# RMSNorm and matmul: TensorE's instructions put in a loop of sixteen tiles, pairs of tiles in three PSUM banks

## The chip, the cores and the metric

The kernel runs on one core of a Trainium2 chip. The metric is the device time of one execution in microseconds; the figure given is the median of the runs. A profile shows one execution, from its first to its last instruction. TensorE (PE) multiplies matrices and writes its results to PSUM. VectorE (DVE) and ScalarE (ACT) work on SBUF and read PSUM. GpSimd (POOL) works on SBUF. SyncE (SP) only issues transfers here. Sixteen DMA engines carry every transfer between DRAM and SBUF, and also the engines' instructions.

## The reference

```python
batch, seq, dim, out_dim = 16, 1024, 512, 768
rms = np.sqrt(np.mean(x ** 2, axis=-1, keepdims=True) + eps)
x_norm = x / rms * gamma
return np.matmul(x_norm, weight).astype(np.float32)
```

`x` is (16, 1024, 512), `weight` (512, 768), all float32. So 33.6 MB of x are read and 50.3 MB of result are written.

## The kernel before, in words

The 16384 rows are 128 tiles of 128 rows, and two tiles are a pair `j` (0 to 63). `gamma` is multiplied into the weights once, which become `w_bf` in bfloat16. The division by the root mean square is left to the end: the product of the raw x and `w_bf` is multiplied by `rstd`, one number a row.

The path of a tile:

- SP loads x in groups of 16 tiles (`load`, line 174; some groups as two transfers of 8) into one of two buffers `xt`. `load_until` is called at the top of each pair and issues a group's load when the pair is 17 or fewer pairs short of it; in SP's order it stands behind the store ahead of it.
- ACT squares and sums each tile (`square`, line 189) and takes the root for a group of pairs (`root`, line 198); DVE takes the reciprocal.
- POOL casts x to bfloat16 (`cast`, line 184, into `xb`).
- PE transposes the tile, two bfloat16 as one 32-bit word, 2 words a tile (`transpose_word`, line 225) into one of the two PSUM banks 6 and 7 (`tp`). It does so for the pair two ahead, in between the products of the present pair (`feeder`, line 324). DVE copies the result to `xT` (`evac`, line 234). The last four tiles of each group of 16 from the second on (a "quad") go another way: POOL casts them into `xq`, and DVE transposes blocks of 32 x 32 from there into `xTq` in 16 moves (`cast_quad` and `move_quad`, three moves a pair). So in six of eight pairs PE has four transposes beside its products, and in two it has none.
- PE multiplies: for each of 4 slices of the features one weight load of `xT` (`hold`, line 294) and two products against `w_bf`, 512 and 256 columns wide (`product`, line 297; `matmuls`, line 305). The result of one tile takes two PSUM banks, one of them half used. Three such accumulators (banks 0 to 5, `ops`) are used in turn, so a tile waits for the scaling of the tile three before it.
- ACT scales the even tiles and DVE the odd ones from PSUM into `ot` (`finish_tile`, line 316; `scale`, line 276). `ot` has three buffers of 8 tiles.
- SP stores 8 tiles as one transfer of 3 MB (`store`, line 287); the first and last groups are split. The scaling of a store's last tile waits for that of the tile before it, so that the store has one wait.

What sets the order: every operation is added to a list with the names of what it reads and writes (`Order.add`). `Order.emit` (line 39) goes through the list once, finds for each operation on whom it must wait, gives each engine one semaphore that counts its awaited operations and each transfer one of a few others, and issues all operations in list order. Each engine runs its own operations in that order, fully written out: TensorE's stream has all 128 tiles in it. The loop over pairs starts in line 404, and its last lines are

```python
for i, engine in ((2 * j, ACT), (2 * j + 1, DVE)):
    a = accumulator()
    matmuls(i, a, range(K), feed)
    finish_tile(i, a, engine)
```

Of the kernel before, what the change touches and what calls it, by code (L numbers as in the profile page):

```python
# [11 lines left out]
F32 = mybir.dt.float32  # L12
BF16 = mybir.dt.bfloat16
# [3 lines left out]
P = 128  # L17
# [3 lines left out]
class Order:  # L21
# [1 line left out]

    def __init__(self, tc):  # L30
        self.tc, self.ops = tc, []

    def add(self, proc, engine, issue, reads=(), writes=()):
        self.ops.append((proc, engine, issue, list(reads), list(writes)))

    def transfer(self, engine, issue, reads=(), writes=()):
# [1 line left out]

    def emit(self):
        nc = self.tc.nc  # L40
        streams = {id(e): n for n, e in enumerate((nc.tensor, nc.vector, nc.scalar, nc.gpsimd, nc.sync))}
        writer, readers = {}, {}
        known = [dict() for _ in streams]
        clocks, needs, place, slot_of, slots = [], [], [], {}, []
        count = [0] * len(streams)
        for n, (proc, engine, _, reads, writes) in enumerate(self.ops):
            at = streams[id(engine)]
            if proc is None:
                me, turn = ("transfer", n), 1
            else:  # L50
                count[at] += 1
                me, turn = at, count[at]
            written = {writer[cell] for cell in reads + writes if cell in writer}
            read = {d for cell in writes for d in readers.get(cell, ())}
            need = []
            for d in sorted(written | read, reverse=True):
                who, when = place[d]
                if who == me and (engine is nc.tensor or d not in written):
                    continue
                if known[at].get(who, 0) < when:  # L60
                    need.append(d)
                    for k, v in clocks[d].items():
                        known[at][k] = max(known[at].get(k, 0), v)
            if proc is None:
                free = [k for k, d in enumerate(slots) if known[at].get(("transfer", d), 0)]
                if free:
                    slots[free[0]] = n
                else:
                    slots.append(n)
                slot_of[n] = ("slot", slots.index(n))  # L70
            clock = dict(known[at])
            clock[me] = turn
            place.append((me, turn))
            clocks.append(clock)
            needs.append(need)
            for cell in reads:
                readers.setdefault(cell, []).append(n)
            for cell in writes:
                writer[cell], readers[cell] = n, []
        awaited = {d for need in needs for d in need}  # L80
        seen = {who for clock in known for who in clock}
        last = [n for n, (me, _) in enumerate(place) if me not in seen and not isinstance(me, int)]
        sems, marks, done = {}, {}, {}
        for n in range(len(self.ops)):
            me = slot_of.get(n, place[n][0])
            if n in slot_of or n in awaited:
                if me not in sems:
                    sems[me] = self.tc.alloc_semaphore(f"done{len(sems)}")
                done[me] = done.get(me, 0) + (16 if n in slot_of else 1)
                marks[n] = (sems[me], done[me])  # L90
        for n, (proc, engine, issue, _, _) in enumerate(self.ops[:-1]):
            for d in needs[n]:
                engine.wait_ge(*marks[d])  # L93
            ins = issue()
            if n in marks:
                ins.then_inc(marks[n][0], 16 if n in slot_of else 1)
        return [marks[n] for n in last if n < len(self.ops) - 1], self.ops[-1][2]


@with_exitstack  # L100
def kernel(
# [9 lines left out]
    PE, DVE, ACT, POOL, SP = nc.tensor, nc.vector, nc.scalar, nc.gpsimd, nc.sync  # L111
    order = Order(tc)

    def run(engine, issue, reads=(), writes=()):
        order.add(1, engine, issue, reads, writes)

    x = x.flatten_outer_dims()
    out = out.flatten_outer_dims()
# [36 lines left out]
    xb = [sb(f"xb{n}", [P, 8, D], BF16) for n in range(2)]  # L155
    jk = [sb(f"jk{n}", [P, D], BF16) for n in range(2)]
    xT = [sb(f"xT{n}", [P, 2, 2, P, 2], BF16) for n in range(4)]
    xq = [sb(f"xq{n}", [P, 4, D], BF16) for n in range(2)]
    xTq = [sb(f"xTq{n}", [P, 4, 2, P, 2], BF16) for n in range(2)]
    ot = [sb(f"ot{n}", [P, OG, O], F32) for n in range(3)]  # L160
    ssq = sb("ssq", [P, NT], F32)
    rms = sb("rms", [P, NT], F32)
    rstd = sb("rstd", [P, NT], F32)
    psum = nc.alloc_psum_tensor("ps", [P, 8 * WIDE], F32).ap()
    ops = [psum[:, 2 * WIDE * n:2 * WIDE * (n + 1)] for n in range(3)]
    tp = [psum[:, WIDE * n:WIDE * (n + 1)].rearrange("p (t h m) -> p t h m", t=2, h=2) for n in (6, 7)]

    def cells(name, slot, i, n=1):
# [65 lines left out]
    def evac(j, t=0, n=2):  # L234
        b = bank(j, t)
        src = tp[b].rearrange("p t h m -> p t (h m)").bitcast(BF16)
        dst = xT[j % 4].rearrange("p t h m c -> p t (h m c)")
        run(DVE, lambda: DVE.tensor_copy(out=dst[:, t:t + n, :], in_=src[:, t:t + n, :]),  # L238
            [("tp", b)], cells("xT", j % 4, t, n))
        for a in range(t, t + n):  # L240
            xT_of[2 * j + a] = (xT[j % 4][:, a], ("xT", j % 4, a))

    def transpose_tile(i):
        for h in range(2):
# [10 lines left out]

    def cast_quad(q):
        src, of = x_of(4 * q, 4)
        s = 4 * q // XG % 2
        run(POOL, lambda: POOL.tensor_copy(out=xq[s], in_=src), of, [("xq", s)])  # L259
        for t in range(4):  # L260
            xT_of[4 * q + t] = (xTq[s][:, t], ("xTq", s))
        words = xq[s].rearrange("p t d -> p (t d)").bitcast(F32).rearrange("p (a w) -> p a w", w=P)
        turned = xTq[s].rearrange("p t h m c -> p (t h m c)").bitcast(F32).rearrange("p (a m) -> p a m", m=P)
        for tokens in range(0, P, B):
            for features in range(0, P, B):
                quad_moves.append((turned[features:features + B, :, tokens:tokens + B],
                                   words[tokens:tokens + B, :, features:features + B], s))

    def move(dst, src, s):
        run(DVE, lambda: DVE.transpose(out=dst, in_=src), [("xq", s)], [("xTq", s)])  # L270

    def move_quad(n):
        for _ in range(min(n, len(quad_moves))):
# [5 lines left out]
        else:  # L279
            run(DVE, lambda: DVE.tensor_single_scalar(out=dst, in_=src, scalar=r, op=mybir.AluOpType.mult), reads, writes)  # L280

    turns = iter(range(NT + 1))

    def accumulator():
        return next(turns) % 3

    def store(i):
        first, n = o_first[i], o_size[i]
# [8 lines left out]
    def product(dst, lhsT, rhs, start, stop, reads, writes):  # L297

        run(PE, lambda: PE.add_instruction(mybir.InstMatmult(  # L299
            name=nc.get_next_instruction_name(), engine=mybir.EngineType.PE,  # L300
            ins=[PE.lower_ap(rhs), PE.lower_ap(lhsT)], outs=[PE.lower_ap(dst)],
            start_tensor_calc=start, stop_tensor_calc=stop, tile_size=(P, P), tile_position=(0, 0), ldweights=False)),
            reads, writes)

    def matmuls(i, a, ks, feed=None):
        block, cell = xT_of[i]
        for k in ks:
            lhsT = block[:, k // 2, :, k % 2]
            hold(lhsT, cell)
            for half, lo, hi in ((0, 0, WIDE), (1, WIDE, O)):  # L310
                product(ops[a][:, lo:hi], lhsT, w_bf[:, k, lo:hi], k == 0, k == K - 1,
                        [cell, ("w", k, half)], [("ops", a, half)])
            if feed:
                feed()

    def finish_tile(i, a, engine):
        s = i // OG % 3

        before = [("ot", s, i % OG - 1)] if i == o_first[i] + o_size[i] - 1 else []
        scale(engine, ot[s][:, i % OG, :], ops[a][:, :O], rstd[:, i:i + 1],  # L320
              [("ops", a, 0), ("ops", a, 1), ("rstd", i)] + before, [("ot", s, i % OG)])
        store(i)

    def feeder(pairs, gaps, alone=False):
# [18 lines left out]
    def load_weights(h):  # L343
# [10 lines left out]
    run(POOL, lambda: POOL.memset(ident_f, 0.0), [], ["ident"])  # L354
    run(POOL, lambda: POOL.affine_select(out=ident_f, in_=ident_f, compare_op=mybir.AluOpType.not_equal, fill=1.0, base=0,
                                         pattern=[[-1, P]], channel_multiplier=1), ["ident"], ["ident"])
    spare = accumulator()

    def warm_up(n):
        hold(warm[:, :P], "warm")  # L360
        for _ in range(n):
            product(ops[spare][:, :WIDE], warm[:, :P], warm, True, True, ["warm"], [("ops", spare, 0)])

    def weights(k, engine, lo=0, hi=O):
        halves = [half for half in range(2) if lo <= half * WIDE < hi]
# [19 lines left out]
    weights(0, DVE, 0, WIDE)  # L385
    weights(0, DVE, WIDE, O)
    weights(1, ACT)
    acc = [accumulator() for _ in range(2)]
    for i in range(2):
        matmuls(i, acc[i], [0, 1])  # L390
    weights(2, DVE)
    weights(3, ACT)
    norms(2, 2)
    cast(4, 2)
    matmuls(0, acc[0], [2, 3])
    finish_tile(0, acc[0], ACT)
    matmuls(1, acc[1], [2, 3], feeder([1], [2, 2], alone=True))
    finish_tile(1, acc[1], DVE)
    cast(6, 2)


# [2 lines left out]
    for j in range(1, NP):  # L404
# [20 lines left out]
            feed = feeder([j + 2], two)  # L425
        else:
            feed = None
        for i, engine in ((2 * j, ACT), (2 * j + 1, DVE)):
            a = accumulator()
            matmuls(i, a, range(K), feed)  # L430
            finish_tile(i, a, engine)


    with tc.tile_critical():  # L434
# [45 lines left out]
```

## Time and profile before

| what | value |
|---|---|
| median of 3 runs | 209.27 us (208.94 to 209.97) |
| profiled execution, first to last instruction | 207.5 us |
| TensorE busy, granted clock | 193.3 us (93%), 0.992 |
| DVE, ACT, POOL busy | 149.3, 144.5, 59.8 us |
| DMA, data queue's share of 16 engines | 97.3%, 85.46 MB |
| DMA, instruction queues | 7 packets and 0.11 MB; 5 packets and 0.04 MB |

The profiled execution's own time outside the profile is not given; its span is 1.77 us under the median of the runs. In the page, a group row gives line, engine, operation, output and input, count, busy time and mean, then the engine's idle time before such instructions and who ended it. A row of the waits is "who waited <- for whom: us in total, times, longest". In the timeline a row is start, duration, engine, and in square brackets the idle time before it. Matmul records stand under the line of the helper that adds them, L299 (products), L229 (transposes) and L295 (weight loads).

### The profile page before, as it was taken

The numbers are of one execution on the slowest core, as the hardware profiler recorded it, in microseconds if no ns is written. First come the engines' busy times: TensorE is split into PE (matmuls) and PEld (weight loads), VectorE is DVE, ScalarE is ACT, GpSimd is POOL, SyncE is SP. The second block draws the span as 40 slices with busy tenths as digits, with TensorE's granted clock in tenths as the row PEclk, the third lists the DMA queues.
The fourth block names the chain that finished last, engine by engine and source line by source line (L and its number), as shares of the span: only waits on it lengthen the run. The fifth ranks groups of instructions, "written<-read, shape, count | busy, mean of one in ns | idle before, by whom it ended". The sixth has DMA issues, their size and how long they took to land.

```text
span 207.5 us, 2761 instructions
## 1 busy us (share of the span) xinstructions
PE 193.3 (93%) x1212; PEld 72.6 (35%) x717; DVE 149.3 (72%) x255; ACT 144.5 (70%) x343; POOL 59.8 (29%) x34
## 2 busy tenths in 40 slices
PE   7779999999999999998999999999999999999940
PEld 1233434433443334342333333443334334433210
DVE  0446556999579966999379984999579984999530
ACT  4698897868777596763977877687867787683310
POOL 2156733009400291003900570006700175000000
PEclk9999999999999999999999999999999999999996
DMA  6999999999999999999999999999999999998993
GB/s 225 403 441 436 388 405 456 455 388 422 436 445 442 395 425 448 429 411 431 434 407 436 437 428 434 418 428 437 417 426 426 433 442 425 426 436 381 407 404 139
DMA packets 5632, 85.62 MB, mean 413 GB/s; under 512 B 626, under 2 KB 628, under 8 KB 1780
## 3 DMA queue, kind: packets, MB, share of 16 engines
q1 hardware_dynamic: 5616, 85.46, 97.3%
q8 instruction: 7, 0.11, 0.2%
q14 instruction: 5, 0.04, 0.0%
q10 hardware_dynamic: 4, 0.00, 0.0%
HBM read 35.13 MB, written 50.33 MB: 412 GB/s over the span
## 4 chain that ended last, share of the span: by engine, by line
PE 71%; DMA 16%; DVE 5%; issue 2%; SPq 1%; ACT 1%; POOL 1%; ACTq 0%
PE ps L299 62%; DMA xt<-in_x_dram 16%; PE ps L229 8%; DVE ot L280 2%; DVE xTq L270 2%; DVE xT L238 1%; SPq L344 1%; POOL xb L187 1%; ACT jk L195 0%; SPq L176 0%; ACT ot L278 0%; SPq L292 0%; DVE rstd L202 0%; SPq L475 0%; ACTq L93 0%
## 5 line engine op out<-in xcount | busy, mean ns | idle before, releaser
L299 PE MATMUL ps<-w_bf,xT 128*128 128x256 bf16 (+1 forms) x783 | 145.0, 325 | 3.4 <-ACT ot L278 1.3
L278 ACT ACTIVATE ot<-ps,rstd 128x768 f32<-128x768 f32 x64 | 57.4, 898 | 42.4 <-PE ps L299 40.5
L195 ACT ACTIVATE jk<-xt 128x512 bf16<-128x512 f32 x128 | 78.8, 619 | 8.3 <-DMA xt<-in_x_dram 8.2
L187 POOL CAST xb<-xt 128x2048 bf16<-128x2048 f32 (+3 forms) x21 | 46.3, 2218 | 113.2 <-DMA xt<-in_x_dram 111.4
L280 DVE TENSOR_SCALAR ot<-ps,rstd 128x768 f32<-128x768 f32 x64 | 64.8, 1013 | 9.9 <-PE ps L299 9.2
L295 PEld LDWEIGHTS <-xT 128*128 128x128 bf16 x400 | 39.3, 98 | 61.2 <-issue 53.2
L229 PE MATMUL ps<-ident_f,xb 128*128 128x128 f32 x200 | 54.4, 277 | 0.9 <-POOL xb L187 0.9
L238 DVE COPY xT<-ps 128x1024 bf16<-128x1024 bf16 (+1 forms) x53 | 34.5, 653 | 24.5 <-PE ps L229 22.8
L270 DVE STREAM_TRANSPOSE xTq<-xq 32x256 f32<-32x256 f32 x112 | 48.7, 435 | 3.4
L229 PEld LDWEIGHTS ps<-ident_f,xb 128*128 128x128 f32 x200 | 28.3, 143 | 46.5 <-issue 42.9
L299 PE MATMUL ps<-w_bf,xTq 128*128 128x256 bf16 (+1 forms) x217 | 41.8, 324 | 0.4
L195 ACT ACTIVATION_READ_ACCUMULATOR jk<-xt 128x1 f32 x128 | 24.3, 190 | 0.0
L295 PEld LDWEIGHTS <-xTq 128*128 128x128 bf16 x112 | 11.0, 98 | 14.5 <-issue 14.5
L259 POOL CAST xq<-xt 128x2048 bf16<-128x2048 f32 x7 | 13.3, 1893 | 0.0
L202 DVE RECIPROCAL rstd<-rms 128x8 f32<-128x8 f32 (+3 forms) x20 | 3.8, 192 | 7.9 <-ACT rms L200 7.7
L200 ACT ACTIVATE rms<-ssq,eps_sb 128x8 f32<-128x8 f32 (+3 forms) x20 | 6.0, 300 | 0.6
L299 PE MATMUL ps<-warm 128*128 128x512 bf16 x10 | 4.4, 582 | 1.4 <-DVE eps_sb L353 1.4
L278 ACT ACTIVATE w_bf<-w_f,g_sb 128x768 bf16<-128x768 f32 x2 | 1.9, 936 | 1.7 <-DMA w_f<-in_weight_dram 1.7
L376 DVE COPY g_sb<-ps 128x4 f32<-128x4 f32 x1 | 0.2, 163 | 3.2 <-PE ps L370 3.2
L340 ACT ACT_TABLE_LOAD x1 | 1.3, 1283 | 1.5 <-SPq L434 1.5
L280 DVE TENSOR_SCALAR w_bf<-w_f,g_sb 128x512 bf16<-128x512 f32 (+2 forms) x3 | 1.4, 481 | 1.1 <-DMA w_f<-in_weight_dram 1.1
L370 PEld LDWEIGHTS ps<-ident_f,g_row 2*128 2x128 f32 x2 | 0.3, 200 | 2.6 <-issue 2.6
(10 smaller groups left out, 2.0 us busy)
## 6 DMA issues: line engine op xcount, KB each, us to landing
out_dram<-ot SPq DMA_DIRECT2D x13, 3072.0 KB, 16.6
xt<-in_x_dram SPq DMA_DIRECT2D x9, 2048.0 KB, 21.1
xt<-in_x_dram SPq DMA_DIRECT2D x3, 4096.0 KB, 22.2
out_dram<-ot SPq DMA_DIRECT2D x4, 1536.0 KB, 11.3
out_dram<-ot SPq DMA_DIRECT2D x3, 768.0 KB, 7.0
w_f<-in_weight_dram SPq DMA_DIRECT2D x2, 768.0 KB, 5.8
xt<-in_x_dram SPq DMA_DIRECT2D x2, 512.0 KB, 5.2
xt<-in_x_dram SPq DMA_DIRECT2D x1, 1024.0 KB, 9.0
```

The source lines that it names most:

```text
L187: run(POOL, lambda: POOL.tensor_copy(out=xb[s][:, i % 8:i % 8 + n, :], in_=src), of, cells("xb", s, i % 8, n))
L195: run(ACT, lambda: ACT.activation(out=jk[j], in_=src[:, 0, :], func=AF.Square, accum_out=ssq[:, i:i + 1]), of, [("jk", j), ("ssq", i)])
L200: run(ACT, lambda: ACT.activation(out=rms[:, s], in_=ssq[:, s], func=AF.Sqrt, scale=1.0 / D, bias=eps_sb), [("ssq", t) for t in range(i, i ...
L202: run(DVE, lambda: DVE.reciprocal(out=rstd[:, s], in_=rms[:, s]), [("rms", i)], [("rstd", t) for t in range(i, i + n)])
L229: run(PE, lambda: PE.transpose(out=tp[b][:, t, h, :], in_=words[:, lo:lo + P], identity=ident_f), cells("xb", s, j % 4 * 2 + t) + ["ident" ...
L238: run(DVE, lambda: DVE.tensor_copy(out=dst[:, t:t + n, :], in_=src[:, t:t + n, :]), [("tp", b)], cells("xT", j % 4, t, n))
L259: run(POOL, lambda: POOL.tensor_copy(out=xq[s], in_=src), of, [("xq", s)])
L270: run(DVE, lambda: DVE.transpose(out=dst, in_=src), [("xq", s)], [("xTq", s)])
L278: run(ACT, lambda: ACT.mul(out=dst, in_=src, mul=r), reads, writes)
L280: run(DVE, lambda: DVE.tensor_single_scalar(out=dst, in_=src, scalar=r, op=mybir.AluOpType.mult), reads, writes)
L295: run(PE, lambda: PE.ldweights(lhsT), [cell])
L299: run(PE, lambda: PE.add_instruction(mybir.InstMatmult(name=nc.get_next_instruction_name(), engine=mybir.EngineType.PE, ins=[PE.lower_ap(r ...
```

## The change

TensorE's part of pairs 6 to 61 (tiles 12 to 123) becomes a hardware loop of 7 turns on TensorE alone. One turn is 8 pairs, 16 tiles. The other engines' instructions stay written out, one after another. For the loop all turns must be alike, in buffers and in semaphore counts, and this is what the other parts of the change do:

- **PSUM.** A pair takes three banks: the first tile columns 0 to 767 of them, the second columns 768 to 1535, so the middle bank holds parts of both tiles. Two such sets (banks 0 to 2 and 3 to 5) alternate from pair to pair. Tiles 0 and 1 and the last four tiles have places of their own, in one case the transposes' banks 6 and 7. The second tile's products are 256 and then 512 columns wide.
- **Scaling.** Both tiles of a pair are scaled after the products of both, by ACT for even pairs and by DVE for odd pairs. The last four tiles are scaled as before.
- **Buffers.** `xq` and `xTq` have one buffer instead of two; pairs 6 and 7, which are transposed by PE, go to `xTq`, where the loop's body looks for the quad.
- **Semaphores.** An operation for which the loop's body waits (a cast, copy, last move or scaling) counts up a semaphore of its engine and of that half of the turn (four pairs), and no other. PE waits for constants on it, and a later product of the same half takes the half's count off again. Whoever else waits for such an operation (a store for a scaling, say) waits for the next operation of the same engine that is not of this kind (`shared`). One small ACT operation is added behind pair 58 so that there is one.
- **Loop head.** The loop's first instruction is placed on the first slot of an instruction fetch block (`head_slot`).

The core of the diff:

```diff
+        for t in turns:
+            for q, (n, half) in enumerate(self.body[t]):
+                for who in waits[q]:
+                    d = direct[n][who]
+                    assert events.setdefault(d, (t, half)) == (t, half)
...
+        def shared(d):
+            if d not in events:
+                return d
+            return next(e for e in order[place[d][0]] if e > d and e not in events)
...
+        for (who, half), sem in own.items():
+            final = max(q for q, w in values if w == who and self.body[turns[0]][q][1] == half)
+            q = next(q for q in range(final + 1, size) if q not in flags and q not in taken and self.ops[self.body[turns[0]][q][0]][0] == "product")
+            taken[q] = (sem, -counts[who, half])
+
+        def give(n):
+            _, engine, issue, _, _ = self.ops[n]
             for d in needs[n]:
-                engine.wait_ge(*marks[d])
+                engine.wait_ge(*marks[shared(d)])
             ins = issue()
             if n in marks:
                 ins.then_inc(marks[n][0], 16 if n in slot_of else 1)
+            elif n in events:
+                ins.then_inc(own[place[n][0], events[n][1]], 1)
...
+        with nc.Fori(0, len(turns), engines=[mybir.EngineType.PE], head_slot={mybir.EngineType.PE: 0}):
+            for q, (n, half) in enumerate(self.body[turns[0]]):
+                for who in waits[q]:
+                    nc.tensor.wait_ge(own[who, half], values[q, who])
+                ins = self.ops[n][2]()
+                if n in marks:
+                    ins.then_inc(marks[n][0], 1)
+                elif q in taken:
+                    ins.then_inc(*taken[q])
+        for n in late:
+            give(n)
...
-    xq = [sb(f"xq{n}", [P, 4, D], BF16) for n in range(2)]
-    xTq = [sb(f"xTq{n}", [P, 4, 2, P, 2], BF16) for n in range(2)]
+    xq = sb("xq", [P, 4, D], BF16)
+    xTq = sb("xTq", [P, 4, 2, P, 2], BF16)
...
-    def accumulator():
-        return next(turns) % 3
+    def accumulator(i):
+
+        j = i // 2
+        if i < 2:
+            return 3 * WIDE * i, WIDE
+        if j >= NP - 2:
+            return (3 * WIDE, 6 * WIDE, 0, 3 * WIDE)[i - 2 * (NP - 2)], WIDE
+        u = (j - 1) % 2
+        return (3 * WIDE * u, WIDE) if i % 2 == 0 else (3 * WIDE * u + O, O - WIDE)
...
+        if i == o_first[i] + o_size[i] - 1:
+            others = [t for t in range(o_first[i], i) if scaled_by[t] is not engine]
+            before = [("ot", s, t % OG) for t in others[-1:]]
...
-        for i, engine in ((2 * j, ACT), (2 * j + 1, DVE)):
-            a = accumulator()
-            matmuls(i, a, range(K), feed)
-            finish_tile(i, a, engine)
+        order.turn, order.half = ((j - 6) // 8, (j - 6) % 8 // 4) if 6 <= j < NP - 2 else (None, 0)
+        if j < NP - 2:
+            for i in (2 * j, 2 * j + 1):
+                matmuls(i, range(K), feed)
+            for i in (2 * j, 2 * j + 1):
+                finish_tile(i, DVE if j % 2 else ACT)
+            if j == NP - 6:
+                run(ACT, lambda: ACT.mul(out=jk[0][:, :1], in_=eps_sb, mul=1.0), ["eps"], [("jk", 0)])
+        else:
+            for i, engine in ((2 * j, ACT), (2 * j + 1, DVE)):
+                matmuls(i, range(K), feed)
+                finish_tile(i, engine)
```

## The prediction

> **What bounds the kernel now.** I read the page from the top: busy shares, the forty slices, the DMA queues.
>
> ```profile
> span 207.5 us, 2761 instructions
> ...
> PE 193.3 (93%) x1212; PEld 72.6 (35%) x717; DVE 149.3 (72%) x255; ACT 144.5 (70%) x343; POOL 59.8 (29%) x34
> ...
> DMA  6999999999999999999999999999999999998993
> ...
> q1 hardware_dynamic: 5616, 85.46, 97.3%
> q8 instruction: 7, 0.11, 0.2%
> q14 instruction: 5, 0.04, 0.0%
> ```
>
> Two resources are nearly full: TensorE (93%) and the DMA engines (97.3% with data). The reader should see that the DMA row never falls below 9 tenths between the first slice and the tail, and that instructions travel on the same engines: seven packets of 16 KB on queue 8, 0.2% x 16 x 207.5 / 7 = about 0.95 us each. In the packet records they begin at 27.1, 50.1, 76.5, 103.5, 127.1, 151.0 and 175.9 us.
>
> Next, the windows (columns: PE, PEld, DVE, ACT, POOL busy; clock; DMA share; GB/s), the longest waits, and the timeline around the one gap in PE.
>
> ```profile
> 47.00:72.00 25.00, 24.84 (x160) 9.37 (x93) 20.62 (x34) 18.21 (x45) 7.87 (x4) 1.00 1.01 430
> 95.00:118.00 23.00, 21.56 (x140) 8.21 (x82) 17.31 (x30) 17.26 (x43) 9.01 (x4) 1.00 1.00 427
> 188.60:207.50 18.90, 10.68 (x66) 3.13 (x32) 7.81 (x11) 3.60 (x4) 0.00 (x0) 0.91 0.78 326
> ```
> ```profile
> PE ps L299 <- ACT ot L278: 1.3, 1, 1.3
> ```
> ```profile
> 96.83 0.63 ACT L195 ACTIVATE jk<-xt 128x512 bf16<-128x512 f32 x1 [3.59 <-DMA xt<-in_x_dram]
> 96.86 5.44 POOL L187 CAST xb<-xt 128x4096 bf16<-128x4096 f32 x2 [18.18 <-DMA xt<-in_x_dram]
> ...
> 98.07 0.88 ACT L278 ACTIVATE ot<-ps,rstd 128x768 f32<-128x768 f32 x1
> ...
> 99.00 1.46 PE L299 MATMUL ps<-w_bf,xT 128*128 128x512 bf16 x8 [1.28 <-ACT ot L278]
> ```
> ```profile
> SPq L475 <- DMA out_dram<-ot: 5.5, 1, 5.5
> ```
>
> PE stands still once after the start, 1.28 us, because a load of x landed at 96.74 and ScalarE squares before it scales. Otherwise PE is full to 199.35. The end is something else: SP waits 5.5 us for the last store. That store is issued at 200.69. Its sixteen engines report completion between 203.91 and 206.63: twelve by 204.38, then 205.35, 205.92, 206.03, 206.63. The twelve have waited for TensorE's last tiles; the last engine has worked without a pause. At the store issued at 178.15 its share lands 4.8 us after the first engine's, and it is late from one disturbance after another of about 1.1 us. So the end is the slowest DMA engine's backlog, and the path through PE has 206.63 - 203.91 = 2.7 us to spare. The span ends 0.9 us later; the median of the runs, 209.27, is 1.77 us above the profiled span, and I add 1.77 to whatever span comes out.
>
> **The change, part by part.**
>
> *Fewer instruction fetches.* Stores are issued at 48.70, 72.12 and 95.54, so sixteen tiles take 23.42 us. They are 16 x 12 products and weight loads and 6 pairs x 4 transposes x 2, 240 instructions. From the first fetch to the last are 148.8 us, less the stall 147.5: 147.5 / 23.42 x 240 / 6 = 252 instructions a fetch, so with some waits a 16 KB block is 256 of 64 bytes. The loop body, 240 plus an add, a branch and few extra waits, fits one block, and its head is put on a block's first slot. With the code before it (12 tiles, 8 transposed pairs, warm-up: 225 instructions) PE needs two to four blocks in all; one or two fetches remain, near 27 us, and five or six go. What is that worth? In the landings each fetch delays another engine by about 1.1 us: the eleventh engine's lag goes from 0.82 to 1.89 around 103.5, the eighth's from 0.68 to 1.78 around 151. The fetches from 103.5 on hit engines that were not last; the last engine's lag is 4.28 before the fetch at 103.5 and 4.29 after it. The last engine seems to hold the one at 27.1, which stays. Bounds for the end: 0, if the last engine keeps all it has, and 1.1, if it loses one disturbance (the three engines behind it, at 206.03 and below, then hold the gain to 0.6 unless they lose one too). I take -0.6.
>
> *The PE stall.* Per group the rows below give DVE and ACT.
>
> ```profile
> L280 DVE TENSOR_SCALAR ot<-ps,rstd 128x768 f32<-128x768 f32 x64 | 64.8, 1013 | 9.9 <-PE ps L299 9.2
> L278 ACT ACTIVATE ot<-ps,rstd 128x768 f32<-128x768 f32 x64 | 57.4, 898 | 42.4 <-PE ps L299 40.5 <-DVE ot L280 1.6
> L238 DVE COPY xT<-ps 128x1024 bf16<-128x1024 bf16 x47 | 32.1, 684 | 23.6 <-PE ps L229 22.0
> L270 DVE STREAM_TRANSPOSE xTq<-xq 32x256 f32<-32x256 f32 x112 | 48.7, 435 | 3.4
> ```
>
> With the same landing ACT squares until 98.05 and scales the pair until 99.85. The pair after next starts at 98.85 and needs the shared bank: about 0.9 us of stall; then the transposes wait for the cast, 96.86 + 3.6 = 100.46, some 0.45 us. Together 1.3: unchanged, and off the ending path by the 2.7 us. If the load lands 1.2 us earlier it is gone.
>
> *One engine scales a pair.* The same 64 + 64 operations in another order. A pair takes 3.04 us on PE, 2.6 without transposes. In a pair that DVE scales it does 3 moves (1.3), one copy (0.7) and two scalings (2.03): 4.0 us, and in the other 2.0. Laying them out from the end of pair 3 of a turn (T): its copy is ready 0.45 before T but follows the moves, ends at T + 0.35; scalings to T + 2.4; pair 5, which takes over the banks, needs the shared one at T + 2.6 + 0.2. Slack 0.4 us, the least of the eight; the others have 1.0. For ACT: two scalings 1.8 of 2.6 us, slack 1.0 where x has landed. So cost 0; if the cover of 0.4 went in every turn, each 0.1 us beyond it is 0.7 us over seven turns, still inside the 2.7. In the first pairs ACT has four squares of 0.61 in pairs 3, 5 and 6; it ends scaling pair 6 at about 34.8, pair 8 wants the banks at 35.0: covered, barely.
>
> *Stores and loads go out later.* A group's last tile was scaled 1.05 us after its pair ended. Now it is the second scaling, and the store waits on the DVE operation after it (a move, 0.44), since the scaling's own count serves the loop: T + 2.6, and 1.5 later than before; where a pair without a move follows, 1.7. Behind that store SP holds the next loads of x. What hides it is the backlog: when a store is issued the transfer ahead of it has this long to run on the fastest engine: 2.6 (48.7), 3.4 (72.1), 4.2 (95.5), 3.7 (120.4), 4.5 (143.8), 5.4 (167.2), 1.8 (178.1), 0.2 (190.7), and 2 to 5 us more on the last one. An issue needs 1.35 before its first byte (200.69 + 1.35 + 8 x 0.23 = 203.9). So the fast engines idle up to 1 us at three places and the last engine not at all. Cost 0 at the end. The last four tiles are scaled one by one as before.
>
> *One buffer for xq and xTq instead of two.* The cast now waits for the moves of the quad before, done two pairs earlier, and on a reciprocal; it ends by about 2 us after pair 6, and DVE takes the first move 2 us after pair 7: covered.
>
> *The loop itself.* No row shows a branch inside PE's stream. Bounds: 0, if the sequencer is ahead of the array; above, a turn that begins with an exposed fetch: 1.35 + 0.95 = 2.3 us x 7 = 16. I take 0 to 1.5, near the first end, because the waits at the loop's head are satisfied 0.8 us before PE arrives and that is queue to work from; all of it fits in the 2.7.
>
> [...]
>
> Sum: 207.5 - 0.6 = 206.9 span, + 1.77 = 208.7; rounded towards the gain side, since five or six disturbances go and none is added: 208.6.
>
> **The rivals.**
> A, the forecast: the slowest engine still sets the end, 208.2 to 209.6. Chance 0.50.
> B, the fetches mattered more: two or more of the late engines lose one, the load lands before 95.5, the stall goes, and the end drops to where all engines are merely full (each packet at the median time of its size makes 199.3 per engine, from 2.1, plus about 1 us of idling and the ending): 205 to 206.4 of span, 206.8 to 208.2. For it: seven disturbances of about 1.1 us. Against: the lags show them on engines that did not end last. 0.27.
> C, the late issues and a new scatter of disturbances give the last engine one more: +1.1, 209.6 to 211. For it: nothing fixes which engine is hit. 0.11.
> D, the other side: the back edge finds its block gone and fetches again, 2.3 us exposed in each of seven turns. PE's path is 203.9 + 16 + 0.9 = 221 of span, 222.6. It decides from 2.7 / 7 = 0.4 us a turn; then the loop saves no fetches either. For it: no branch measured. Against: 240 of 256. 0.08.
> E, DVE's two scalings eat their 0.4 us of slack by more than 0.4 in each turn: from 7 x 0.4 = 2.8 it shows, 210.5 to 213. 0.04.
>
> **How the numbers follow.** No change can be told from one of 0.5% (1.05 us): faster is below 208.2, slower above 210.3. Faster: B and a fifth of A, 0.37. Slower: half of C, D, E: 0.18. Same: 0.45. The range 206.8 to 210.8 leaves out the fastest of B (0.05) and D, E and the top of C (0.13).
>
> **What will show it.** Queue 8 with one or two packets (seven or more: D). PE's waits with the same single entry of about 1.3 us on ACT or POOL, or none (B). A wait on DVE or ACT of a few tenths recurring every 23.4 us is E; PE idle with no releaser at the turns is D. SP's stores 1.5 us later after the pair's end and DMA still 9 throughout. SP's last wait still about 5.5 us says that the slowest engine ends the run; near 3.2 says that TensorE does. I am wrong if PE's path grows by more than 2.7 us, or if the last engine's lateness came from the fetches after all.

## The result, and the profile after

The changed kernel takes 211.91 us (211.74 to 212.10, 4 runs) against 209.17 us (208.94 to 209.97, 4 runs): a ratio of 1.0134, 95% interval 1.0106 to 1.0161. It is 2.7 us slower, above the range that was forecast. The profiled execution has a span of 209.9 us and a time of 211.74 us.

The page of the changed kernel, with the lines that answer to those shown of before:

```profile
span 209.9 us, 2767 instructions
...
PE 193.4 (92%) x1212; PEld 75.9 (36%) x717; DVE 149.1 (71%) x256; ACT 141.3 (67%) x343; POOL 60.2 (29%) x34
...
DMA  6999999998999899999999999999999999999991
GB/s 230 429 440 434 365 392 471 425 409 376 450 371 412 329 445 445 435 443 393 432 428 434 448 421 426 423 434 431 440 426 418 434 421 445 435 417 420 421 404 46
...
q1 hardware_dynamic: 5616, 85.46, 96.8%
q8 instruction: 3, 0.05, 0.1%
q14 instruction: 5, 0.04, 0.0%
```

TensorE is busy as long as before and the instruction fetches fell from seven to three, so the loop is there and works. What is new is in the last digits of the DMA row and in the row of GB/s: a slice is 5.2 us, and the tenth (47 to 52 us) falls to 8 tenths and 376 GB/s, while the twelfth and the fourteenth (58 to 63 and 68 to 73 us) fall to 371 and 329 GB/s with 9 and 8 tenths still busy (422, 445 and 395 GB/s before). All three lie around the store of tiles 16 to 23 and the 4 MB load behind it. After 73 us nothing of the kind follows.

TensorE's waits in the changed kernel (us in total, times, longest):

```profile
PE ps L375 <- DVE eps_sb L436: 1.4, 1, 1.4
PE ps L375 <- DVE xTq L307: 1.0, 1, 1.0
PE ps L294 <- POOL xb L252: 0.6, 1, 0.6
PE ps L375 <- DVE w_bf L347: 0.5, 1, 0.5
PE ps L375 <- DVE xT L307: 0.5, 1, 0.5
PE ps L375 <- ACT ot L345: 0.4, 1, 0.4
```

There is no recurring wait, neither at the loop's back edges nor for the scalings, and the stall of 1.28 us at 97.7 us is gone. The one new wait above 0.5 us is the second row. TensorE's timeline shows it where the loop is entered:

```profile
29.69 0.50 PE L375 MATMUL ps<-w_bf,xTq 128*128 128x512 bf16 x2 [1.05 <-DVE xTq L307]
```

SyncE's timeline around the store of tiles 16 to 23, first of the kernel before, then of the changed one:

```profile
48.70 0.33 SPq L292 DMA_DIRECT2D out_dram<-ot  x1
49.07 0.46 SPq L176 DMA_DIRECT2D xt<-in_x_dram  x1
```
```profile
51.19 0.33 SPq L368 DMA_DIRECT2D out_dram<-ot  x1
51.56 0.43 SPq L241 DMA_DIRECT2D xt<-in_x_dram  x1
```

The store is issued 2.49 us later. The transfer ahead of it lands its first share at 51.29 us before and at 51.25 us after, so of the 2.59 us of work that the fastest DMA engine had left at the issue, 0.07 us is left. (Work left is counted to that landing here and below.) Between 50.8 and 52.2 us the sixteen engines now idle 13.1 engine-us, that is microseconds added up over the engines, 0.8 us each. That, however, is the smaller part. The windows show the rest (columns as in the prediction; the last two are the DMA share and GB/s), before and after:

```profile
51.00:53.00 2.00, 2.00 (x15) 0.64 (x8) 1.36 (x3) 2.00 (x5) 2.00 (x2) 1.00 1.00 418
57.00:62.00 5.00, 4.95 (x34) 1.93 (x19) 3.83 (x7) 4.01 (x10) 0.00 (x0) 1.00 1.03 442
67.00:72.00 5.00, 4.95 (x33) 1.81 (x18) 4.80 (x9) 2.53 (x8) 0.59 (x1) 1.00 0.97 413
```
```profile
51.00:53.00 2.00, 2.00 (x15) 0.68 (x7) 1.48 (x4) 2.00 (x5) 0.73 (x1) 1.00 0.77 324
57.00:62.00 5.00, 5.00 (x35) 2.17 (x20) 2.89 (x5) 3.28 (x10) 0.17 (x1) 1.00 1.05 377
67.00:72.00 5.00, 4.95 (x34) 2.06 (x20) 4.74 (x10) 3.08 (x7) 0.13 (x1) 1.00 0.96 338
```

The first row is the idle time (share 0.77). In the other two the engines are as busy as before (1.05 and 0.96), but the same busy time moves 15% and 18% less: packets take longer where the engines pass from the store to the load (around 60 us) and from the load to the next store (around 70 us). Packets more than 0.1 us over the median time of their size stand in two groups, at 57.5 to 61 and at 67.5 to 70 us; their excess is 14.2 and 13.9 engine-us, 0.9 and 1.4 around the same store before. Together, 13.1 + 14.2 + 13.9 - 0.9 - 1.4 = 39 engine-us, 2.4 us on each of sixteen engines. The landings agree: on the mean of the sixteen engines the transfer ahead lands 0.2 us earlier than before (51.76 against 51.97), the load 2.35 us later (71.36 against 69.01). The first engine is 1.48 us later at 60.17 and 2.85 us later at 71.06, and it keeps 2.8 us up to the store issued at 179.11. At the end the first share lands at 204.61 (203.91 before) and the last at 209.00 (206.63), 2.4 us later, which is the growth of the span. The engine that ends last can be followed in the packet records, since its packets of 24 KB take about 0.945 us and those of the others 0.912: its last one ends at 193.62, 3.07 us later than in the kernel before (190.55), where by the landings two engines were later still.

### The profile page after: what moved, and what is told of

The parts are those of the page before. It is cut to its first block, busy times and chain, and to the rows that moved or that the text cites. A ratio compares the mean times of both kernels' runs of the same rounds, so it can differ in the third digit from the quotient of the medians.

```text
span 209.9 us, 2767 instructions
## 1 busy us (share of the span) xinstructions
PE 193.4 (92%) x1212; PEld 75.9 (36%) x717; DVE 149.1 (71%) x256; ACT 141.3 (67%) x343; POOL 60.2 (29%) x34
## 4 chain that ended last, share of the span: by engine, by line
PE 86%; DMA 3%; ACT 3%; issue 1%; DVE 1%; SPq 1%
PE ps L375 75%; PE ps L294 10%; DMA xt<-in_x_dram 3%; ACT jk L260 1%; ACT ot L345 1%; DVE ot L347 0%; SPq L427 0%; DVE xTq L307 0%; ACT rms L265 0%; DVE xT L307 0%; SPq L241 0%; DVE rstd L267 0%; SPq L563 0%; SPq L522 0%
## 5 line engine op out<-in xcount | busy, mean ns | idle before, releaser
L375 PE MATMUL ps<-w_bf,xT 128*128 128x256 bf16 (+1 forms) x752 | 139.7, 325 | 2.1 <-DVE w_bf L347 0.5
L345 ACT ACTIVATE ot<-ps,rstd 128x768 f32<-128x768 f32 x63 | 53.5, 897 | 48.3 <-PE ps L375 48.3
L347 DVE TENSOR_SCALAR ot<-ps,rstd 128x768 f32<-128x768 f32 x65 | 63.2, 1012 | 6.6 <-PE ps L375 6.2
L371 PEld LDWEIGHTS <-xT 128*128 128x128 bf16 x384 | 37.7, 98 | 55.9 <-issue 39.1
L307 DVE COPY xT<-ps 128x1024 bf16<-128x1024 bf16 (+1 forms) x51 | 33.0, 652 | 23.5 <-PE ps L294 21.9
L375 PE MATMUL ps<-w_bf,xTq 128*128 128x512 bf16 (+1 forms) x248 | 47.9, 324 | 1.1 <-DVE xTq L307 1.0
L260 ACT ACTIVATION_READ_ACCUMULATOR jk<-xt 128x1 f32 x128 | 24.8, 194 | 0.0
L371 PEld LDWEIGHTS <-xTq 128*128 128x128 bf16 x128 | 12.5, 98 | 17.6 <-issue 11.5
L307 DVE COPY xTq<-ps 128x1024 bf16<-128x1024 bf16 x2 | 1.4, 692 | 2.8 <-PE ps L294 2.8
```

The costliest lines, as they stand in the source:

```text
L260: run(ACT, lambda: ACT.activation(out=jk[j], in_=src[:, 0, :], func=AF.Square, accum_out=ssq[:, i:i + 1]), of, [("jk", j), ("ssq", i)])
L345: run(ACT, lambda: ACT.mul(out=dst, in_=src, mul=r), reads, writes)
L371: run(PE, lambda: PE.ldweights(lhsT), [cell])
L375: run(PE, lambda: PE.add_instruction(mybir.InstMatmult(name=nc.get_next_instruction_name(), engine=mybir.EngineType.PE, ins=[PE.lower_ap(r ...
```

## The experiments

The theory, formed from these traces: the late store is the cost. Its lateness lets the DMA queue run short ahead of a 4 MB load, and both the idling and the longer packets follow from that. The rival: the loop is the cost (its entry, its back edges, its fetches), and the bad slices are another effect of it.

**The late store alone, in the kernel before.** The store of tiles 16 to 23 (in a second kernel, of tiles 48 to 55) waits also for the scaling two tiles later; nothing else changes:

```diff
-        if i == first + n - 1:
+        if i == first + n - 1 and i != 23:
...
+        if i == 25:
+            first, n = o_first[23], o_size[23]
...
+                           reads=cells("ot", late, first % OG, n) + [("ot", s, i % OG)])
```

> The kernel before, with one change: the store of tiles 16 to 23 also waits for the scaling of tile 25 and goes out about 2.6 us later, near 51.3 us. TensorE has no loop and the old banks. Starved queue: the transfer engines idle about 1.3 us at 51 us, 211 to 212. The loop, or scatter: 209.2, since neither is touched.

> The kernel before, with the same delay at another store: tiles 48 to 55 wait for the scaling of tile 57, 2.6 us later, near 98.1 us, where the transfer ahead still has 4.2 us to run. Starved queue: covered, 209.0 to 209.5. Rival, a late store costs its delay wherever it stands: 211 to 212.

The first takes 210.38 us, ratio 1.0077 (1.0049 to 1.0106); the second 209.36 us, 1.0024 (1.0008 to 1.0040). In the first the store is issued at 50.76 with 0.52 us of work left, and the engines idle 5.4 engine-us. Its windows:

```profile
51.00:53.00 2.00, 2.00 (x15) 0.71 (x7) 1.23 (x3) 1.93 (x6) 2.00 (x2) 1.00 0.96 397
57.00:62.00 5.00, 4.95 (x34) 2.04 (x20) 4.23 (x7) 3.61 (x10) 0.00 (x0) 1.00 1.03 375
67.00:72.00 5.00, 4.95 (x33) 1.81 (x19) 4.81 (x9) 1.50 (x3) 0.00 (x0) 1.00 1.02 351
```

The 375 and 351 GB/s of the changed kernel are there without any other part of the change: one store 2.06 us late costs 1.6 us (1.0 to 2.2), less than the theory had expected. The second kernel makes a store 1.8 us late that still finds 2.50 us of work ahead of it; it costs 0.5 us (0.2 to 0.8). (Behind it stand two loads of 2 MB instead of one of 4 MB.) So lateness alone is cheap, and a short queue is dear.

**The loop undone.** The changed kernel with TensorE's seven turns written out; everything else, the later stores included, stays:

```diff
-        with nc.Fori(0, len(turns), engines=[mybir.EngineType.PE], head_slot={mybir.EngineType.PE: 0}):
-            for q, (n, half) in enumerate(self.body[turns[0]]):
+        for t in turns:
+            for q, (n, half) in enumerate(self.body[t]):
```

> The changed kernel with its seven turns written out one after another; banks, scaling and semaphores stay. Starved queue: the entry gap of 1.05 us goes, the store of tiles 16 to 23 is issued near 50.1 instead of 51.2 and the transfer engines idle some 0.3 us instead of 1.2; seven fetches are back; 209.3 to 210.3. The loop as the whole cause: 209.2. Scatter: nothing fixes it, 209 to 212.

210.46 us, 1.0072 (1.0050 to 1.0094), with seven fetches again. That is what the late store alone cost in the kernel before. Its store is issued at 50.71 with 0.50 us left, and its windows at the load's ends read 370 and 357 GB/s. So the new order of scaling, the shared wait and the single buffers, which together make this store 2.0 us late, cost about 1.5 us, no more than the late store by itself; and the loop costs about 1.3 us more (1.0134 against 1.0072). For TensorE's entry into the loop this kernel still has a wait:

```profile
29.20 0.50 PE L375 MATMUL ps<-w_bf,xTq 128*128 128x512 bf16 x2 [0.46 <-DVE xTq L307]
```

So 0.46 of the 1.05 us belongs to the copy into `xTq`, and 0.5 to 0.6 to the loop.

**The loop, but not placed on a block's first slot.** `head_slot` is left out of the `Fori` line:

> The changed kernel without the placing of the loop's head: the body of about 242 instructions then lies over a block's boundary. If a boundary inside the body makes the back edge fetch its block again: 8 or more packets on queue 8, and up to 2.3 us in each turn, 212 to 226. If both blocks stay: 3 packets, and the entry gap of 1.05 us smaller, 211 to 212.

210.98 us (2 runs), 1.0087 (1.0065 to 1.0110). The gap at the entry is 0.46 us as in the unrolled kernel, the store is issued at 50.67, and queue 8 reads

```profile
q8 instruction: 2, 0.03, 0.1%
```

Two fetches in all, so the seven turns don't each bring one, with a body of some 242 instructions that by the prediction's counts now lies across two blocks. So it is the placing of the head that delays TensorE by half a microsecond (1.05 against 0.46 us; by what means, no run shows), and through the store that lets the queue run from 0.48 us of work to 0.07. By the ratios it accounts for about 1.0 of the loop's 1.3 us (1.0134 against 1.0087, whose intervals overlap a little); the remaining 0.3 us can't be told from nothing. So both theories hold a part, and the loop's part too runs through the late store.

**Giving the queue work: stores in halves.** In the changed kernel the stores of tiles 8 to 15 and 16 to 23 go out as two transfers of four tiles each, so that SyncE can issue the first half some 6 us earlier:

```diff
-    o_first, o_size = stretches(OG, {0: [1, 1, 2, 4], last - 1: [4, 4], last: [4, 2, 2]})
+    o_first, o_size = stretches(OG, {0: [1, 1, 2, 4], 1: [4, 4], 2: [4, 4], last - 1: [4, 4], last: [4, 2, 2]})
```

> Starved queue: the stores of tiles 8 to 15 and 16 to 23 go out in halves, so the transfer engines do not run dry at 51 us; no idle there, PE as in the changed kernel with its one gap of 1.05 us at the loop's entry, time 209.0 to 209.8. Rival, the loop: the time comes with TensorE's loop, 211.9 as before this edit. Rival, scatter: the last engine is late for its own reasons (two fetches near 30 us and slower packets), 211.9 too, with idle at 51 us gone and the last engine still 4 us behind the first.

211.27 us, 1.0109 (1.0081 to 1.0136): little gained, and for an instructive reason. SyncE's timeline:

```profile
11.98 21.06 SPq L368 DMA_DIRECT2D out_dram<-ot  x5
33.08 0.43 SPq L241 DMA_DIRECT2D xt<-in_x_dram  x1
```

The half store of tiles 8 to 11 stands ahead of a load in SyncE's order and waits for its tiles; the load behind it is issued at 33.08 instead of 28.36. The shortage has moved: to this half store (1.13 us of work left) and to the store at 76.23 (0.82 left), and the theory's 209.0 to 209.8 was missed. Next, only the stores that themselves stand ahead of a load with little left were split: that of tiles 16 to 23 (`2: [4, 4]`) in the changed kernel, in the same kernel unrolled, and in the kernel before.

> The changed kernel with only the store of tiles 16 to 23 cut in two halves; the first goes out near 45 us and SP's loads keep their places (in the first edit of this kind a half store stood ahead of a load of x and held it for 4.7 us). Starved queue: the transfer engines have work at 51 us, no idle there, few packets longer than usual at 57 to 71 us (they stood at the two ends of the load behind a store that met an empty queue); 2.4 us less than the changed kernel, 209.0 to 210.0. Scatter as the cause: 211 to 212.

> The same with TensorE's turns written out: the loop alone is the difference to the run above, with the queue never empty in both. If fetches cost the last engine, 0.5 to 1 us slower than with the loop; if the entry gap costs more than the fetches, up to 0.5 faster. I expect 209.3 to 210.3, within 0.7 of the run above.

> The kernel before with the same cut of that one store, as a control: the queue was not empty there, so no change, 208.6 to 209.5. If cutting a store were itself worth time, below 208.

210.10 us, 1.0051 (1.0037 to 1.0066); unrolled 210.10 us, 1.0043 (1.0030 to 1.0056); in the kernel before 209.09 us, 1.0008 (0.9994 to 1.0021). Halves alone do nothing where there is no shortage, and in the changed kernel they give back 1.7 of the 2.7 us. The windows of the changed kernel with this store in halves:

```profile
51.00:53.00 2.00, 2.00 (x15) 0.60 (x7) 1.55 (x4) 2.00 (x5) 0.76 (x1) 1.00 0.99 416
57.00:62.00 5.00, 5.00 (x36) 2.17 (x20) 2.85 (x4) 3.35 (x10) 0.24 (x1) 1.00 1.09 469
67.00:72.00 5.00, 5.00 (x35) 2.07 (x20) 4.74 (x10) 3.63 (x9) 0.81 (x1) 1.00 0.94 397
```

The bad stretches at 51 and 57 us are gone; the next store ahead of a load, at 74.68, now finds 0.79 us of work and pays 2.9 engine-us of idling and 28 in long packets. So the stores of tiles 32 to 39 were split as well (`4: [4, 4]`): with the loop, with the loop unplaced, and unrolled. A last kernel has the loop unplaced and tiles 48 to 55 in halves too (`6: [4, 4]`).

> The changed kernel with the stores of tiles 16 to 23 and 32 to 39 each cut in halves, since cutting the first alone moved the shortage to the next store that stands ahead of a 4 MB load (issued at 74.7 with 0.8 us of work left). Starved queue: at both places more than 2 us of work is left, no idle before 188 us, no groups of long packets at the ends of the loads; 208.3 to 209.3. If something else than the queue costs the 1.1 us that are left: 210.

> The same without the placing of the loop's head, which cost the gap of 1.05 us at the entry and no fetch fewer: PE's path 0.5 to 1 us shorter, two packets on queue 8. 207.8 to 209.0; the version most likely to beat both kernels. If the fetches were worth nothing, equal to the kernel before.

> The same halves with TensorE's turns written out: with no shortage left, the difference to the two runs above is what the loop is worth, five fetches saved. If each fetch delays one engine by 1.1 us and one of the last engines holds one, 0.3 to 1.0 us slower than without the head's placing: 208.5 to 209.5.

> The kernel after, loop not placed on a block's first slot, with the stores of tiles 16 to 23, 32 to 39 and 48 to 55 in halves. The last store that stands ahead of a load with little work left (97.54 us, 2.3 us left in the run with two pairs of halves and no placed head, 5.0 engine-us in packets longer than usual behind it) then finds about 5 us left. Theory 1 (only short work ahead of a load costs time, the loop itself nothing): those long packets go, and the time is that of the unrolled kernel with two pairs of halves, 209.46, between 209.0 and 209.8, which is also the time of the kernel before. Theory 2 (the loop costs some 0.8 us in another way, which these runs don't name): 210.0 to 210.6 as with two pairs of halves. Both expect two or three packets of instructions on queue 8 and no wait of TensorE's over 0.6 us between 24 and 190 us.

| kernel | us | ratio to before, 95% |
|---|---|---|
| loop, two stores in halves | 210.28 | 1.0053 (1.0037 to 1.0069) |
| loop not placed, two stores in halves | 210.28 | 1.0045 (1.0030 to 1.0061) |
| unrolled, two stores in halves | 209.46 | 1.0015 (1.0002 to 1.0028) |
| loop not placed, three stores in halves | 210.49 | 1.0054 (1.0034 to 1.0074) |

The first two rows missed what the theory had expected of them, 208.3 to 209.3 and 207.8 to 209.0. Once no store finds the queue short, the rest of the change (one engine scaling a pair, three banks, single buffers, shared waits) costs nearly nothing: unrolled, 0.3 us is left of 2.7. The loop's saved fetches are worth nothing: with equal stores the unrolled kernel with its seven fetches is as fast (210.10 and 210.10) or faster. In the last row no shortage was left, and it still took 210.49 us: the loop keeps about 1 us (the difference to the unrolled kernel) that short work ahead of a load does not explain.

The first two rows also set a limit to the theory. With the placed head a third store, that of tiles 48 to 55, still finds the queue short: it is issued at 97.98 with 1.82 us of work left, against 97.54 and 2.32 without the placing. Behind it come 21.8 engine-us in long packets against 5.8, which the windows at the end of the load show (first with the placed head, then without):

```profile
114.00:118.00 4.00, 4.00 (x29) 1.70 (x17) 3.77 (x9) 2.91 (x7) 2.35 (x1) 1.00 1.06 346
114.00:118.00 4.00, 4.00 (x27) 1.62 (x15) 3.74 (x10) 3.20 (x7) 2.31 (x1) 1.00 1.07 426
```

The 16 engine-us more are 1 us on each engine, and the mean landing of the second load is 1 us later with the placed head (119.1 against 118.1); the last landing is not (121.26 against 121.41), and both kernels take 210.28 us. So long packets don't pass one for one into the time, which the last engine sets.

As to the loop's 1 us: with one store in halves it doesn't show (210.10 both), with two or three it does. In the profiled runs the first DMA engine's share of the last store lands alike, 203.82 us in the last kernel and 203.81 in the unrolled one, and the last engine's 4.18 and 2.77 us behind it. What makes the slowest engine lag more there stayed open. Over all fourteen profiles the last engine's lag behind the first, at the last 3 MB store, is no different with the loop (mean 4.2 us of seven) than without (4.1 of seven), so seven fetches did not make the last engine later than two or three. No version beat the kernel before.

Over these runs the packet records can be ordered by one number: the work that the first-finishing DMA engine has left when a store directly ahead of a load is issued. The load is of 4 MB, or two of 2 MB where the table says so.

| kernel | store issued, us | work left, us | idle, engine-us | long packets, first and second group, engine-us |
|---|---|---|---|---|
| kernel before | 72.12 | 3.41 | 0 | 0.6 + 2.8 |
| before, tiles 16 to 23 in halves | 72.29 | 3.15 | 0 | 0.6 + 2.1 |
| kernel before | 48.70 | 2.59 | 0 | 0.9 + 1.4 |
| before, tiles 48 to 55 late (two loads) | 97.34 | 2.50 | 0 | 1.3 + 3.3 |
| changed, loop not placed, two stores in halves (two loads) | 97.54 | 2.32 | 0 | 0.2 + 5.6 |
| changed, two stores in halves (two loads) | 97.98 | 1.82 | 0 | 5.9 + 15.9 |
| changed, unrolled, tiles 16 to 23 in halves | 73.92 | 1.58 | 0 | 3.2 + 15.4 |
| changed, tiles 8 to 23 in halves | 32.71 | 1.13 | 0.1 | 11.5 + 16.4 |
| changed, tiles 8 to 23 in halves | 76.23 | 0.82 | 2.5 | 13.0 + 18.5 |
| changed, tiles 16 to 23 in halves | 74.68 | 0.79 | 2.9 | 11.8 + 16.6 |
| before with tiles 16 to 23 late | 50.76 | 0.52 | 5.4 | 12.7 + 17.9 |
| changed, unrolled | 50.71 | 0.50 | 6.7 | 14.1 + 15.3 |
| changed, loop not placed | 50.67 | 0.48 | 6.3 | 15.2 + 14.7 |
| changed | 51.19 | 0.07 | 13.1 | 14.2 + 13.9 |

These are all nine such stores of the fourteen profiles (from 28 us on) that found less than 2.3 us, and five of the 62 that found more; behind none of the 62 do engines idle, and the long packets are at most 5.8 engine-us. Idling begins between 1.13 and 0.82 us of work left. The long packets begin earlier, between 2.32 and 1.82 us, and then cost 19 to 32 engine-us, 1.2 to 2 us on every engine, whether or not an engine idles. Why the packets lengthen isn't settled. That the engines run in step afterwards is not enough for it: between 86 and 95 us of the changed kernel they are within 0.7 us of each other and no packet of the load is long.

## Why the prediction was wrong

Step by step, in its own words:

- *What bounds the kernel: right.* The slowest DMA engine still sets the end. SyncE's last wait in the changed kernel, 5.5 us before:

```profile
SPq L563 <- DMA out_dram<-ot: 8.2, 1, 8.2
```

  TensorE's path did not grow: the last store is issued at 200.40 instead of 200.69.
- *Fewer instruction fetches: the count was near (three, not one or two), the worth of -0.6 us was not found.* Its lower bound, 0, was the better value.
- *The PE stall: gone instead of unchanged,* since the load landed 0.76 us earlier (95.98 us) and TensorE came later; as said, it lies off the ending path and gained nothing.
- *One engine scales a pair: right.* No recurring wait on DVE or ACT; the slack of 0.4 us held in all seven turns.
- *One buffer for xq and xTq: right for the cast* (a row "POOL xq" waits 8.5 us in five goes and delays nobody); but the copy into `xTq` ahead of the loop gave TensorE 0.46 us that had not been counted.
- *The loop itself: inside its bounds, and with a consequence that wasn't drawn.* No back edge shows (no wait of TensorE's stands between 31 and 200 us). The entry costs 0.5 to 0.6 us, which does fit in the 2.7 us that TensorE's path had to spare; but it makes the next store late, and that was not in the sum.
- *Stores and loads go out later: this is the step that failed.* "Cost 0 at the end", because "the fast engines idle up to 1 us at three places and the last engine not at all". Two errors stand in it. The lateness at the store with 2.6 us of work ahead was 2.49 us instead of 1.5 to 1.7, as 0.46 us of the copy and 0.5 us of the loop's entry came on top; at one place ahead of a load, 0.8 us of idling on each engine was the result. And the idling was taken to be the whole price, paid by engines that end early. In its place the runs showed a second price that falls on all engines, the last one too: 28 engine-us in longer packets where the engines pass from the store to the load and at the load's end. The late store alone, put into the kernel before, cost 1.6 us where the step said 0. The step's "1.35 before its first byte" is also read wrongly: where engines stood idle, the first packets start 0.83 to 0.95 us after the issue, and the rest is the 0.3 to 0.5 us by which a landing is recorded behind the end of its last packet.
- The premise beneath that step was weak as well: the last engine's lag of 2 to 5 us was taken as a fixed reserve. In the changed kernel all sixteen engines land within 0.67 us at 60 us, everyone late, and the engine that ends last gathers its lag anew: 0.84 us at 110 us, 4.17 at 190 us, mostly in steps of about 0.3 us a transfer. So at 121 us the last landing was still no later than before (120.94 against 121.04), because in the kernel before other engines were last there; the loss shows at the end because the slow engine had lost it too.

Of the rivals, C had the sign and the word (late issues), but its 209.6 to 211 ends below what was measured, and a single engine's 1.1 us is not what happened: every engine lost. B is refuted by the unrolled kernels, which are no slower with seven fetches (210.10 against 210.10 us, 209.46 against 210.28), D by the three packets on queue 8, E by TensorE's waits. What was expected of the unplaced loop as its worse case, a fetch at each back edge and 8 or more packets, did not come either: some 242 instructions, across two blocks by the prediction's counts, with two packets in all. At the seven turns of the changed kernel the records of TensorE's sequencer show a compare-and-branch of 207 to 240 ns (76 ns at the last), and none of them shows as a wait of TensorE's.

## What to carry to other kernels

Where the DMA engines bound a kernel, count for each store that stands ahead of a load how much work the queue still has at its issue, and add up all the delays that reach this one issue (a later scaling, a wait on another operation, a loop head's half microsecond), also those that the computing engine can afford. Once that work was nearly used up here (below about 2 us), the price was more than the idle time (28 engine-us in longer packets beside 13.1 of idling in the changed kernel); a store in two halves gave part of it back (1.7 of the 2.7 us), where the first half did not stand ahead of a load that it then held up. Fewer instruction fetches were no gain by themselves (two stores in halves: 210.28 us with two or three, 209.46 with seven).

## What the runs showed of the hardware that was not expected

- Where a store ahead of a load was issued with 1.8 us of work left or less, packets took longer, most of them by 0.15 to 0.9 us each: the store's last and the load's first, and again the load's last some 10 us later. It is 18.6 to 31.5 engine-us in the nine lower rows of the table, against at most 5.8 at the 62 stores with 2.3 us or more.
- From a store's issue on SyncE to its first packet on an idle DMA engine it was 0.83 to 0.95 us in six of these runs.
- One DMA engine wrote slower than the others: its lag grew by about 0.3 us in most 3 MB stores (0.945 against 0.912 us, 33 ns, for each of its 8 packets of 24 KB). In the changed kernel, whose engines had been brought into step, it is the one that ends last.
- The loop on TensorE whose body of some 242 instructions is not placed on a block's first slot made two fetches in the whole execution (two packets on queue 8), fewer than its seven turns, and placing its head there cost 0.5 us of TensorE at the entry (1.05 us of idle time against 0.46).
